# A log-softmax over rows of 50000: one row on eight partitions, fp32 in place, eight buffers, transfers from SyncE

## The chip, the cores and the metric

The kernel runs on one core of a Trainium2 chip; the other cores are idle. The metric is the device time of one execution in microseconds (us), as the slowest core shows it; with one core there is only that one. Wherever two kernels are compared, each was run on the same chip in alternation with the kernel before.

## The reference

```python
batch, seq, vocab = 16, 512, 50000          # x: fp32, 1638.4 MB
max_x = np.max(x, axis=-1, keepdims=True)
shifted = x - max_x
log_sum_exp = np.log(np.sum(np.exp(shifted), axis=-1, keepdims=True))
return (shifted - log_sum_exp).astype(np.float32)
```

There are 8192 rows of 50000 values. Each row needs its maximum, then the sum of its exponentials, then a subtraction from every value. Every byte is read once and written once if a row stays on the chip in between.

## The kernel before

A tile is 128 whole rows, one row per partition, held as bf16 (100 KB per partition, two such tiles). The load converts on its way, and so does the store.

```python
res_pool = ctx.enter_context(tc.tile_pool(name="res", bufs=2))
for it in range(ntiles):                                   # 64 tiles of 128 rows
    xres = res_pool.tile([P, V], bf16)
    for j in range(4):
        nc.gpsimd.dma_start(out=xres[:, c0:c0+LOAD_C], in_=xf[...])   # 128x12500, fp32 -> bf16
    # ... four reduce_max on VectorE, one more over the four: negmax
    for j in range(20):
        nc.scalar.activation(out=scratch, in_=xres[...], func=Exp,    # 128x2500
                             bias=negmax, accum_out=psum[:, j:j+1])
    # ... reduce_sum, Ln (another table), neglse = negmax - logsum
    for j in range(4):
        nc.scalar.activation(out=xres[...], in_=xres[...], func=Identity, bias=neglse)
        nc.gpsimd.dma_start(out=of[...], in_=xres[...])               # bf16 -> fp32
```

## Time and profile before

| | before |
|---|---|
| median time | 9335.58 us (9335.44 to 9335.72, 3 runs) |
| ScalarE (ACT) busy | 6053.9 us, 65% |
| VectorE (DVE) busy | 3400.9 us, 36% |
| DMA engines | 82.5% of 16 engines' span |
| HBM traffic | 1638.4 MB read, 1638.4 MB written |

Read it from the bottom: the traffic is fixed by the task, the DMA engines are the busiest unit, and yet they are not busy all the time. The question is when they are idle and what they then wait for.

### The profile page before, as it was taken

To read this page: it belongs to the slowest core of one execution; us is meant where nothing else is said; L and a number is where in the kernel's file an instruction comes from. 1 tells how busy PE (TensorE), PEld (TensorE's weight loads), DVE (VectorE), ACT (ScalarE), POOL (GpSimd) and SP (SyncE) were. 2 spreads that over 40 slices of the span, in tenths; PEclk is the share of its full clock that TensorE was granted. 3 is DMA by queue.
4 is the path that set the end of the run, shared out by engine and by line. 5 is a ranking of instruction groups with operands and counts; after the bars stand their busy time and mean duration, and the time that the engine had idled before them with its cause. 6 is when DMAs were issued, how large, how long until landed. Compare 5 with 4: busy or idle time off the path is not lost.

```text
span 9333.9 us, 4650 instructions
## 1 busy us (share of the span) xinstructions
DVE 3400.9 (36%) x448; ACT 6053.9 (65%) x3008; POOL 272.8 (3%) x516
## 2 busy tenths in 40 slices
DVE  4432334323344234442344423444224442243422
ACT  6556865568655686556865568655686556865568
POOL 0000000000000000000000000000000000000000
DMA  8797787977879778898778987789877888778886
GB/s 230 237 299 276 262 245 242 295 276 265 240 246 289 278 267 237 250 285 281 271 230 257 278 285 271 226 261 274 286 276 223 264 267 290 276 223 267 261 293 255
DMA packets 73765, 2457.94 MB, mean 263 GB/s; under 512 B 8192, under 2 KB 8192, under 8 KB 8192
## 3 DMA queue, kind: packets, MB, share of 16 engines
q0 software_dynamic: 73728, 2457.63, 82.5%
q14 instruction: 37, 0.30, 0.0%
HBM read 1638.40 MB, written 1638.40 MB: 351 GB/s over the span
## 4 chain that ended last, share of the span: by engine, by line
ACT 55%; DVE 18%; DMA 15%; issue 10%; another core or an unknown queue 2%; POOL 0%; ACTq 0%; POOLq 0%; PEldq 0%
ACT scratch L71 29%; ACT xres L95 26%; DVE pmax L56 18%; DMA xres<-in_x_dram 15%; ACT L83 1%; ACT L71 0%; POOL out_dram L102 0%; ACTq L131 0%; ACT logsum L83 0%; DVE neglse L91 0%; DVE negmax L63 0%; POOL xres L48 0%; POOLq L131 0%; PEldq L131 0%
## 5 line engine op out<-in xcount | busy, mean ns | idle before, releaser
L71 ACT ACTIVATE scratch<-xres,negmax 128x2500 bf16<-128x2500 bf16 x1280 | 3042.5, 2377 | 3216.6 <-DVE negmax L63 3177.9
L56 DVE TENSOR_REDUCE pmax<-xres 128x1 f32<-128x12500 bf16 x256 | 3372.5, 13174 | 2597.9 <-DMA xres<-in_x_dram 2597.9
L95 ACT ACTIVATE xres<-xres,neglse 128x12500 bf16<-128x12500 bf16 x256 | 2720.6, 10697 | 7.3 <-DVE neglse L91 7.3
L81 DVE TENSOR_REDUCE ssum<-psum 128x1 f32<-128x20 f32 x64 | 11.1, 174 | 3091.5 <-ACT scratch L71 3091.5
L102 POOL DMA_DIRECT2D out_dram<-xres x256 | 136.4, 533 | 7275.5 <-ACT xres L95 7250.2
L71 ACT ACTIVATION_READ_ACCUMULATOR scratch<-xres,negmax 128x1 f32 x1280 | 238.6, 186 | 0.0
L48 POOL DMA_DIRECT2D xres<-in_x_dram x256 | 136.4, 548 | 1752.2 <-DMA out_dram<-xres 1745.9
L71 ACT ACT_TABLE_LOAD x64 | 82.1, 1283 | 20.3 <-DMA xres<-in_x_dram 19.2
L83 ACT ACT_TABLE_LOAD x64 | 82.1, 1283 | 1.1
L91 DVE TENSOR_TENSOR neglse<-negmax,logsum 128x1 f32<-128x1 f32 x64 | 10.2, 160 | 165.9 <-ACT logsum L83 165.9
L83 ACT ACTIVATE logsum<-ssum 128x1 f32<-128x1 f32 x64 | 13.0, 203 | 0.7
L63 DVE TENSOR_REDUCE negmax<-pmax 128x1 f32<-128x4 f32 x64 | 9.7, 152 | 1.1
L120 POOL MEMSET const-float32-0.0<- 128x1 f32 x1 | 0.1, 98 | 0.2 <-issue 0.2
L120 POOL MEMSET const-bfloat16-1.0<- 128x1 bf16 x1 | 0.1, 101 | 0.0
L120 POOL MEMSET const-float32-1.0<- 128x1 f32 x1 | 0.1, 98 | 0.0
L120 POOL MEMSET const-uint8-127<- 128x1 uint8 x1 | 0.1, 98 | 0.0
## 6 DMA issues: line engine op xcount, KB each, us to landing
out_dram<-xres POOLq DMA_DIRECT2D x256, 6250.0 KB, 21.8
xres<-in_x_dram POOLq DMA_DIRECT2D x256, 3125.0 KB, 64.8
```

Of the source, the lines that this page charges most:

```text
L48: nc.gpsimd.dma_start(out=xres[:, c0 : c0 + LOAD_C], in_=xf[r0 : r0 + P, c0 : c0 + LOAD_C],)
L56: nc.vector.reduce_max(out=pmax[:, j : j + 1], in_=xres[:, c0 : c0 + LOAD_C], axis=mybir.AxisListType.X,)
L63: nc.vector.reduce_max(out=negmax, in_=pmax, axis=mybir.AxisListType.X, negate=True)
L71: nc.scalar.activation(out=scratch, in_=xres[:, c0 : c0 + C_EXP], func=mybir.ActivationFunctionType.Exp, bias=negmax, scale=1.0, accum_out ...
L81: nc.vector.reduce_sum(out=ssum, in_=psum, axis=mybir.AxisListType.X)
L83: nc.scalar.activation(out=logsum, in_=ssum, func=mybir.ActivationFunctionType.Ln, bias=0.0, scale=1.0,)
L91: nc.vector.tensor_sub(out=neglse, in0=negmax, in1=logsum)
L95: nc.scalar.activation(out=xres[:, c0 : c0 + OUT_C], in_=xres[:, c0 : c0 + OUT_C], func=mybir.ActivationFunctionType.Identity, bias=neglse ...
L102: nc.gpsimd.dma_start(out=of[r0 : r0 + P, c0 : c0 + OUT_C], in_=xres[:, c0 : c0 + OUT_C],)
L120: nc = _bacc.Bacc("TRN2", target_bir_lowering=False, num_devices=1)
```

## The change

The intent is to keep the DMA engines always at work. A row is cut into 8 pieces on 8 neighbouring partitions, so a tile is only 16 rows (128x6250 fp32, 3.2 MB, contiguous in HBM), and there are eight such buffers. Nothing is converted, and the transfers are issued by SyncE instead of GpSimd. The price is that a row's maximum and sum must be combined over 8 partitions.

```diff
+G = 8
+R = P // G
+EXP_C = 3125
+NBUF = 8
+AHEAD = 5
...
+    xt = xf.rearrange("(t r) (g w) -> t (r g) w", r=R, g=G)
+    data = ctx.enter_context(tc.tile_pool(name="data", bufs=NBUF))
...
+    # ones: 128x128, ones in 8x8 blocks on the diagonal (GpSimd, once)
+    nc.scalar.preload_act_table_set("natural_log_exp_and_others")
+    def load(t):
+        buf = data.tile([P, W], FP32, name="buf")
+        nc.sync.dma_start(out=buf, in_=xt[t])
+    def front(t):
+        nc.vector.reduce_max(out=pmax, in_=buf, axis=AX)
+        nc.vector.transpose(out=allmax, in_=pmax.to_broadcast([P, SQ]))
+        nc.vector.tensor_reduce(out=rowmax, ..., op=ALU.max, axis=AX, negate=True)
+        nc.vector.tensor_copy(out=spread..., in_=rowmax... .to_broadcast(...))
+        nc.vector.transpose(out=negmax, in_=spread)
+        for j in range(nexp):                       # 2 pieces of 3125
+            nc.scalar.activation(out=dump, in_=buf[...], func=ACT.Exp,   # dump in PSUM
+                bias=negmax[:, 0:1], scale=1.0, accum_out=part[:, j : j + 1])
+        for j in range(nexp):
+            nc.tensor.matmul(rowsum, ones, part[:, j : j + 1], ...)
+        nc.scalar.activation(out=logsum, in_=rowsum, func=ACT.Ln)
+    def back(t):
+        nc.vector.tensor_scalar(out=buf, in0=buf, scalar1=shift.pop(t)[:, 0:1],
+            scalar2=logs.pop(t), op0=ALU.add, op1=ALU.subtract)
+        nc.sync.dma_start(out=ot[t], in_=buf)
+    for t in range(AHEAD):
+        load(t)
+    for t in range(ntiles + 1):                     # 512 tiles
+        if t + AHEAD < ntiles:
+            load(t + AHEAD)
+        if t < ntiles:
+            front(t)
+        if t >= 1:
+            back(t - 1)
```

SyncE issues its transfers strictly in this order: load t+5, store t-1, load t+6, store t, and so on.

## The prediction

> **What bounds the kernel now.** I read the page top down first: busy shares, slices, DMA queues, groups.
>
> ```profile
> DVE 3400.9 (36%) x448; ACT 6053.9 (65%) x3008; POOL 272.8 (3%) x516
> ...
> DMA  8797787977879778898778987789877888778886
> ...
> q0 software_dynamic: 73728, 2457.63, 82.5%
> ...
> HBM read 1638.40 MB, written 1638.40 MB: 351 GB/s over the span
> ```
>
> No engine is full: ScalarE (ACT) is at 65%, VectorE (DVE) at 36%, the DMA engines at 82.5%. So either something rotates between them, or one of them is full only in stretches. The byte counts matter: the queue carried 2457.63 MB because a load of 6.4 MB of fp32 lands as 3.2 MB of bf16, but HBM still gave and took 1638.40 MB each way, 3276.8 MB in all. Next I read which groups were idle, and for what.
>
> ```profile
> L71 ACT ACTIVATE scratch<-xres,negmax 128x2500 bf16<-128x2500 bf16 x1280 | 3042.5, 2377 | 3216.6 <-DVE negmax L63 3177.9
> L56 DVE TENSOR_REDUCE pmax<-xres 128x1 f32<-128x12500 bf16 x256 | 3372.5, 13174 | 2597.9 <-DMA xres<-in_x_dram 2597.9
> L95 ACT ACTIVATE xres<-xres,neglse 128x12500 bf16<-128x12500 bf16 x256 | 2720.6, 10697 | 7.3 <-DVE neglse L91 7.3
> L48 POOL DMA_DIRECT2D xres<-in_x_dram x256 | 136.4, 548 | 1752.2 <-DMA out_dram<-xres 1745.9
> ```
>
> Four waits close a circle: exp waits 3177.9 us for the maximum, the maximum 2597.9 us for loads, new loads 1745.9 us for stores to free their buffer, and a store for ScalarE's last pass. Two buffers of 128 whole rows are all there is, so both tend to be loading, or both computing or storing. The chain of waits, in order of time, repeats every 290.87 us (2609.36 to 2900.23), two 128-row tiles; 32 such periods are 9308 us of the 9333.9 us span. I cut one period into stretches (columns: stretch, length, DVE, ACT, POOL busy, clock, DMA share, GB/s):
>
> ```profile
> 2653.00:2738.00 85.00, 76.97 (x7) 27.64 (x23) 0.00 (x0) 1.00 1.01 217
> 2740.00:2778.00 38.00, 13.66 (x4) 37.65 (x25) 0.00 (x0) 1.00 0.00 0
> 2780.00:2838.00 58.00, 0.00 (x0) 57.64 (x26) 1.60 (x3) 1.00 1.01 428
> 2856.00:2867.00 11.00, 9.03 (x2) 10.76 (x3) 0.00 (x0) 1.00 0.00 0
> ```
>
> While loading, the DMA engines are full (217 GB/s of bf16 landing is 434 GB/s read from HBM). While storing they are full again, at 428 GB/s. In between, for 38 us and again for 11 us, they carry nothing, and ScalarE works alone. What is lost is DMA time: this kernel is a DMA-limited one with holes.
>
> **The rate of a full DMA.** From the timeline, the maxima of consecutive load pieces start when each lands:
>
> ```profile
> 2652.41 13.18 DVE L56 TENSOR_REDUCE pmax<-xres 128x1 f32<-128x12500 bf16 x1 [72.23 <-DMA xres<-in_x_dram]
> 2667.18 13.17 DVE L56 TENSOR_REDUCE pmax<-xres 128x1 f32<-128x12500 bf16 x1 [1.59 <-DMA xres<-in_x_dram]
> 2682.00 13.17 DVE L56 TENSOR_REDUCE pmax<-xres 128x1 f32<-128x12500 bf16 x1 [1.65 <-DMA xres<-in_x_dram]
> 2696.73 13.17 DVE L56 TENSOR_REDUCE pmax<-xres 128x1 f32<-128x12500 bf16 x1 [1.56 <-DMA xres<-in_x_dram]
> ```
>
> 2667.18 to 2696.73 is two pieces, 14.78 us each; over the first seven (19.18 to 107.70, six steps) it is 14.75 us for 6.4 MB, or 434 GB/s. The period holds 16 transfers (8 loads, 8 stores) of 6.4 MB on the HBM side: 16 x 14.75 = 236 us of 290.87. The other 55 us are the two holes and their edges, and 32 x 55 = 1760 us is about what a kernel without holes could save.
>
> **What the Trainium skill says.** "DMA: Bandwidth & Descriptors", section "Where 436 GB/s comes from", puts the ceiling of the path into SBUF at 435 GB/s; the 434 above agrees. The same page, section "Latency and other measured facts", gives copies from HBM and back 214 GB/s per direction at full rate, so 428 together: loads and stores share one budget. The trace before agrees in its store stretch but scarcely mixes the two. "VectorE: DVE Perf Modes", section "The perf-mode tier table", has a reduction at one element per cycle in any type, and tensor_scalar on fp32 in SBUF at two. The trace agrees on the first (12500 elements in 13174 ns, so 0.96 per ns and some 153 ns fixed); nothing in it shows the second. "ScalarE: Activation LUTs", section "Table sets: the hidden batching unit", says one set holds both exp and ln; before, the trace pays 128 table loads of 1283 ns, 164 us.
>
> **The change, part by part** (per new tile: 16 rows, 128x6250 fp32, 3.2 MB; 512 tiles).
>
> DMA: still 1638.4 MB each way, since the old conversion saved only the SBUF side. One load and one store are 6.4 MB together: 14.75 us at the old load rate, 512 x 14.75 = 7552 us.
>
> VectorE: maximum 6250/0.96 + 153 = 6.66 us. Four small operations of 152 to 174 ns (the small reductions before), with waits about 0.8 us. The subtraction moves here from ScalarE: at two elements per cycle 3255 ns + some 160 = 3.4 us. Sum 10.9 us, below 14.75; 512 x 10.9 = 5580 us busy, some 73%.
>
> ScalarE: the four Identity passes (2720.6 us) go. An exp of 3125 elements costs 2377 + 625 x 0.833 = 2.90 us (slope from 10697 - 2377 ns over 10000 elements, 0.832), and its accumulator read 0.19; two of each 6.2 us, the Ln 0.2: 6.4 us per tile, 3270 us, some 43%. Table loads fall to one. The exp's output goes to PSUM, which may change its fixed part by tens of ns; it is off the path.
>
> TensorE: two 128x1 products per tile sum the 8 partial sums and spread them. I guess 1 us of latency, hidden.
>
> Does a wait replace the one removed? A tile's chain is 7.5 us front, 6.4 us exponentials, about 1 us of sums and Ln, and the subtraction, which VectorE does after the next tile's front: some 20 us. A load is issued five tiles ahead, and waits for the store of the tile three back. When that store lands, the queue still holds one load and one store, 14.75 us of transfers, and the new load needs only some 2 us to be issued and start. The store that follows it has long been computed. So the queue never runs dry. At the start seven loads are queued, 52 us, while the first store is ready after about 30 us. At the end, when the last load lands, some five stores are still queued (37 us) and the last tile's chain is shorter than that. Fill and drain therefore add only first and last latencies, about 5 us.
>
> Sum: 7552 + 5 = 7557 us if mixed transfers run at 434 GB/s. At the 428 of the store stretch, 3276.8 MB take 7656 us. The page's busy share (82.5% of 9333.9 us for 3276.8 MB) makes 425.5 GB/s, 7701 us. Rows of 25000 B rather than 50000 mean twice the descriptors per byte, and direction changes every 7.4 us; I allow a little for each and take 7620 us, or 430 GB/s.
>
> **Rivals.**
> 1. VectorE becomes the bound. If the subtraction runs at one element per cycle it costs 6.7 us and VectorE needs 14.1 us per tile, 7240 us at 95% busy: still just under DMA, with little slack, so 7600 to 7800 us. Doubled small-operation overheads on top would pass DMA: 7700 to 7900. For it: no such fp32 operation in the trace. Against: the tier table.
> 2. Alternating loads and stores is slower than either alone, say 400 GB/s: 8190 us. For it: the trace has long one-way stretches only. Against: the last of four stores and the next load followed each other at the usual pace (first store issued about 2577, landing of the load after all four at 2652.4: five transfers in 75 us, 15 us each), and the 214 GB/s above.
> 3. Loads and stores overlap in the engines, as they use opposite directions of HBM and SBUF; then the time would fall to VectorE's 5600 to 6500 us. Against: the 428 GB/s total above, and shares already at 1.01 in one-way stretches.
> 4. Ordering: loads and stores sit in one in-order SyncE queue, so a load waiting for an old store could hold back a ready one. For it: the program order. Against: the 14.75 us of work queued behind. If it bites, a hole of 1 to 3 us per tile: 8000 to 9000 us.
>
> **Range and chances.** The first sum's rates give 7557 to 7706 us with drain. Rival 1 lies within or just above, 2 and 4 in a tail of one in ten together, 3 about 3%. So 7620 us, with 7540 to 7770 eight times in ten. Being slower needs a loss of 1700 us, more than any rival but the worst makes: faster 0.97, same 0.015, slower 0.015.
>
> **What would show it.** DMA near 10 tenths in every slice and some 430 GB/s throughout; 3276.8 MB on the SyncE queue; VectorE near 73% with the subtraction at about 3.4 us and waiting mainly for loads; ScalarE near 43% with one table load; new loads waiting for old stores, without an empty stretch. A subtraction of 6.7 us would show rival 1, a full DMA at under 415 GB/s rival 2, holes in the DMA share rival 4.

## The result, and the profile after

The changed kernel took 7898.29 us in the median of 4 runs (7884.30 to 7910.61); before took 9335.65 beside it. The ratio is 0.846, with a 95% interval from 0.8448 to 0.8472. (Ratios here are the mean time of one kernel's fast runs over that of the other's fast runs of the same rounds, so not quite the ratio of the medians that are quoted.) It is faster, but 278 us above the predicted 7620, and above the range that ended at 7770. It also varies: 26 us between its fastest and slowest run, against 0.3 us before.

The page of the changed kernel: busy times, then of the 40 equal slices the DMA share in tenths and the GB/s moved, then the SyncE queue.

```profile
PE 600.4 (8%) x2048; PEld 513.0 (6%) x2048; DVE 5566.8 (70%) x3072; ACT 3152.9 (40%) x2561; POOL 1.2 (0%) x7
...
DMA  9999999999999999999999999999999999999999
GB/s 416 426 430 431 431 431 431 431 431 431 431 430 431 429 428 410 410 403 409 409 406 403 404 405 408 407 408 405 409 408 401 406 403 413 408 405 406 406 405 385
...
q1 hardware_dynamic: 147456, 3276.87, 99.9%
```

The holes are gone: every slice has 9 tenths. The third line is the surprise. For 15 slices, some 2960 us, the kernel moves the 430 GB/s that were predicted (a little less in the first two); then it drops within about one slice to some 406 and stays there. The DMA share gives no hint of it. Two windows put numbers on it (columns: stretch, length, busy times of PE, PEld, DVE, ACT and POOL with their instruction counts, clock, DMA share, GB/s):

```profile
1000.00:2600.00 1600.00, 126.23 (x431) 107.81 (x431) 1164.79 (x643) 661.36 (x538) 0.00 (x0) 1.00 1.00 431
3200.00:7800.00 4600.00, 342.43 (x1168) 292.55 (x1168) 3173.53 (x1748) 1797.37 (x1460) 0.00 (x0) 1.00 1.00 406
```

At 406 GB/s, 4600 us carry 1868 MB, which at 431 would have taken 4333 us: 267 us lost here, about the whole distance to the prediction. The groups, answering to those shown of before:

```profile
L81 DVE TENSOR_REDUCE pmax<-buf 128x1 f32<-128x6250 f32 x512 | 3411.6, 6663 | 2231.9 <-DMA buf<-in_x_dram 2231.9
L102 ACT ACTIVATE dump<-buf,negmax 128x3125 f32<-128x3125 f32 x1024 | 2937.9, 2869 | 4370.9 <-DVE negmax L96 4354.4
L117 DVE TENSOR_SCALAR buf<-buf,negmax,logsum 128x6250 f32<-128x6250 f32 x512 | 1789.8, 3496 | 4.5 <-ACT logsum L112 3.6
...
L67 ACT ACT_TABLE_LOAD x1 | 1.3, 1283 | 0.8 <-PEq L146 0.8
```

The engines do what was worked out for them. The maximum takes 6.663 us (6.66 predicted), the exp 2.869 (2.90), the subtraction 3.496 (3.4). VectorE waits 2231.9 us, all of it for loads, so it is not the bound. SyncE, which issues, waits as expected too:

```profile
SPq L75 <- DMA out_dram<-buf: 7333.8, 504, 23.6
SPq L121 <- DVE buf L117: 72.9, 6, 25.0
```

Loads (L75) wait for old stores to free their buffer, 504 times. Stores (L121) waited for VectorE only 6 times. So every transfer is ready early, the queue is held only by buffers, and still the rate falls after 37% of the run. Why there?

The timeline shows it as the time between two loads that SyncE issues, one per tile, first in the fast part and then in the slow part:

```profile
2308.29 0.33 SPq L75 DMA_DIRECT2D buf<-in_x_dram  x1
...
2323.15 0.33 SPq L75 DMA_DIRECT2D buf<-in_x_dram  x1
...
4001.13 0.33 SPq L75 DMA_DIRECT2D buf<-in_x_dram  x1
...
4017.03 0.33 SPq L75 DMA_DIRECT2D buf<-in_x_dram  x1
```

A tile takes 14.86 us in the first pair and 15.90 in the second: 1 us more per tile, with the same work and the same order.

### What the landings say

A transfer runs on 16 DMA engines, each with its own share and its own queue of work (a ring). The Trainium skill, "DMA: Bandwidth & Descriptors", section "Why a DMA increments its semaphore by 16 and not by 1", says that these engines finish independently and that the semaphore counts them. The trace agrees: it has 16 landings for each of the 1024 transfers. Their spread, the time from the first engine's landing to the last one's, is the lag of the slowest ring behind the fastest. Worked out from the landing records of the trace (median over the transfers that landed in the 100 us after each time):

```
lag in us at      300   600  1000  1500  2000  2500  3000  4000  5000  6000  7000 us
before            0.2   0.3   0.2   0.2   0.2   0.2   0.2   0.2   0.5   0.2   0.2
changed           3.9   5.2   7.3   9.1  11.6  11.5  12.7  13.6  13.4  13.6  13.0
```

Before, the rings finish together: each period has idle stretches (38 and 11 us) in which all can catch up, and there are fewer instruction fetches, of which more below (37 packets against 80). In the changed kernel they drift apart, until the lag reaches 12 to 13 us near 3000 us. There it stops growing, and there the rate falls.

That suggests theory 1. The awaited store "lands" only when the slowest ring has done its part. Behind it are two transfers, 14.75 us of work *for each ring*. A ring that is 12.7 us ahead has only 2 us of that left when SyncE hears of the landing, and a new transfer needs about that to be issued and to start (an estimate; in e6 below a tiny load landed 1.6 us after the store that it had waited for, at 1948.6 and 1947.0 us). Slack that is counted on the average ring is used up by the spread between rings.

What makes the rings drift? Up to 2900 us, the lag of the last ring behind the median one rises in clear steps of 1.0 to 1.2 us, at 944, 1213, 1481, 1764, 2032, 2301, 2569 and 2852 us. Every step shows at the landing some 4 us after one 8 KB packet of the instruction queue (309 to 376 ns each), at 940, 1208, 1477, 1760, 2028, 2296, 2565 and 2848 us. These packets bring the engines' own instructions, and the steps say that they pass through the same rings as the data. The interval is 268 us, twice 283, so 18 or 19 tiles; whose instructions they are the packets do not say. VectorE, with 6 operations per tile, is a guess so far.

The rivals: theory 2, that far parts of the two tensors disturb one another (an effect of the address); theory 3, that mixed loads and stores slow down as such, by whatever pattern they happen to fall into.

### The profile page after: what moved, and what is told of

Read it like the earlier page. It is cut to its first block, busy times and chain, and to the rows that moved or that the text cites. A ratio compares the mean times of both kernels' runs of the same rounds, so it can differ in the third digit from the quotient of the medians.

```text
span 7908.9 us, 12333 instructions
## 1 busy us (share of the span) xinstructions
PE 600.4 (8%) x2048; PEld 513.0 (6%) x2048; DVE 5566.8 (70%) x3072; ACT 3152.9 (40%) x2561; POOL 1.2 (0%) x7
## 4 chain that ended last, share of the span: by engine, by line
DMA 97%; SPq 1%; DVE 1%; issue 0%; ACT 0%; PE 0%; ACTq 0%
DMA out_dram<-buf 97%; SPq L75 1%; DVE pmax L81 1%; DMA buf<-in_x_dram 0%; DVE buf L117 0%; ACT dump L102 0%; DVE allmax L84 0%; DVE rowmax L86 0%; DVE spread L91 0%; DVE negmax L96 0%; PE rowsum L108 0%; ACT logsum L112 0%; ACTq L102 0%
## 5 line engine op out<-in xcount | busy, mean ns | idle before, releaser
L81 DVE TENSOR_REDUCE pmax<-buf 128x1 f32<-128x6250 f32 x512 | 3411.6, 6663 | 2231.9 <-DMA buf<-in_x_dram 2231.9
L102 ACT ACTIVATE dump<-buf,negmax 128x3125 f32<-128x3125 f32 x1024 | 2937.9, 2869 | 4370.9 <-DVE negmax L96 4354.4
L117 DVE TENSOR_SCALAR buf<-buf,negmax,logsum 128x6250 f32<-128x6250 f32 x512 | 1789.8, 3496 | 4.5 <-ACT logsum L112 3.6
L108 PE MATMUL rowsum<-part,ones 128*128 128x1 f32 x2048 | 600.4, 362 | 7269.8 <-ACT dump L102 7269.8
L108 PEld LDWEIGHTS rowsum<-part,ones 128*128 128x128 f32 x2048 | 513.0, 311 | 7357.1 <-ACT dump L102 7335.3
L102 ACT ACTIVATION_READ_ACCUMULATOR dump<-buf,negmax 128x1 f32 x1024 | 190.8, 186 | 0.0
L96 DVE STREAM_TRANSPOSE negmax<-spread 128x32 f32<-128x32 f32 x512 | 108.2, 211 | 17.7
L84 DVE STREAM_TRANSPOSE allmax<-pmax 128x32 f32<-128x32 f32 x512 | 108.2, 211 | 17.5
L86 DVE TENSOR_REDUCE rowmax<-allmax 128x4 f32<-128x32 f32 x512 | 95.3, 186 | 17.8
L91 DVE COPY spread<-rowmax 128x32 f32<-128x32 f32 x512 | 92.9, 181 | 17.8
```

Source lines behind the costliest of these rows:

```text
L81: nc.vector.reduce_max(out=pmax, in_=buf, axis=AX)
L84: nc.vector.transpose(out=allmax, in_=pmax.to_broadcast([P, SQ]))
L86: nc.vector.tensor_reduce(out=rowmax, in_=allmax.rearrange("p (r g) -> p r g", g=G), op=ALU.max, axis=AX, negate=True,)
L91: nc.vector.tensor_copy(out=spread.rearrange("p (r g) -> p r g", g=G), in_=rowmax[:, :, None].to_broadcast([P, SQ // G, G]),)
L96: nc.vector.transpose(out=negmax, in_=spread)
L102: nc.scalar.activation(out=dump, in_=buf[:, j * EXP_C : (j + 1) * EXP_C], func=ACT.Exp, bias=negmax[:, 0:1], scale=1.0, accum_out=part[:, ...
```

## The experiments

All kernels are the changed kernel with the edit shown. All gave correct results except e8.

| run | edit | median us (range) | ratio to before |
|---|---|---|---|
| changed kernel | | 7898.29 (7884.30 to 7910.61) | 0.8460 |
| e1 | tiles in reverse order | 7905.78 (7887.76 to 7937.61) | 0.8472 |
| e3 | lookahead 6 | 9760.87 (9750.20 to 9769.78) | 1.0455 |
| e2 | lookahead 4 | 7674.69 (7666.69 to 7679.62) | 0.8220 |
| e5 | lookahead 3 | 7645.33 (7643.27 to 7646.24) | 0.8189 |
| e9 | lookahead 2 | 7772.52 (7736.25 to 7787.42) | 0.8320 |
| e4 | 6 memsets per tile on VectorE | 7982.71 (7977.28 to 7988.96) | 0.8551 |
| e7 | 6 memsets per tile on GpSimd | 8026.63 (8025.42 to 8047.46) | 0.8603 |
| e10 | the same, paced by the tiles | 7907.87 (7895.19 to 7926.23) | 0.8477 |
| e6 | three full stops | 7674.79 (7673.52 to 7675.68) | 0.8221 |
| e8 | loads alone | 3846.8 (one look) | |

### e1: is it the address?

```diff
-        nc.sync.dma_start(out=buf, in_=xt[t])
+        nc.sync.dma_start(out=buf, in_=xt[ntiles - 1 - t])
-        nc.sync.dma_start(out=ot[t], in_=buf)
+        nc.sync.dma_start(out=ot[ntiles - 1 - t], in_=buf)
```

> The tiles are visited from the last to the first, nothing else changes. In the changed kernel the rate falls from 431 to about 406 GB/s near 2900 us and stays there. Theory 1 (ring drift: one of the 16 DMA engines falls behind the others by about 12 us, until the two transfers queued behind the awaited store are used up): the fall comes at about 2900 us again, 7890 to 7920 us in all. Theory 2 (address: loads and stores at the far part of the tensors disturb one another): the slow 406 GB/s comes first and the fast 431 last, with the change at about 5000 us. Theory 3 (mixing as such): no clear order; the step would move or vanish.

The rate by slices:

```profile
GB/s 417 426 429 431 430 431 430 431 431 431 430 429 431 430 427 407 406 407 408 406 405 405 407 406 408 406 403 409 409 404 407 411 406 404 407 407 405 408 406 388
```

The fast part is first again, and the fall comes in the same slice, although the tensors are now walked from the far end. Theory 2 falls.

### e2, e3: how much work lies behind the awaited store?

```diff
-AHEAD = 5
+AHEAD = 4        # e2;   6 in e3
```

With lookahead a, load t+a needs the buffer of tile t+a-8, and the last store issued by then is that of tile t-2. Behind the awaited store there are 6-a pairs of a load and a store: none for 6, two transfers for 5, four for 4, six for 3.

> Loads are issued four tiles ahead instead of five; still eight buffers. A load then waits for the store of four tiles back, with four transfers (29.5 us) queued behind it instead of two. Theory 1 (ring drift, growing at some 3.7 us per 1000 us): the rate stays near 430 GB/s until the lag reaches about 27 us, at 6700 us or later; 7640 to 7680 us in all. Theories 2 (address) and 3 (mixing): the fall near 2900 us stays and the time is 7890 to 7920 us.

> Loads are issued six tiles ahead; a load waits for the store of two tiles back, with one transfer (7.4 us) queued behind it. Theory 1 (ring drift): the fall comes when the lag reaches about 5 us, at 500 to 1300 us, and the time is 7980 to 8080 us. Theories 2 and 3: 7890 to 7920 us, fall near 2900 us as before, since the queue is as deep on average as it was.

e2, then e3, by slices, and a window of e3 with the columns of the windows above:

```profile
GB/s 416 426 431 431 430 430 431 431 431 431 431 431 430 431 431 431 431 430 431 430 431 431 431 431 430 431 431 431 431 431 431 431 430 430 430 430 428 415 410 365
```

```profile
GB/s 357 336 335 334 334 340 334 338 332 337 335 334 334 336 335 335 334 334 336 333 338 335 339 331 335 336 334 335 335 337 340 334 333 333 337 337 334 337 338 351
```

```profile
1000.00:9000.00 8000.00, 491.92 (x1676) 420.36 (x1676) 4555.52 (x2514) 2579.18 (x2095) 0.00 (x0) 1.00 0.88 335
```

e2 met the expectation closely, 7674.69 us where 7640 to 7680 was expected. The fall moved from 2960 us to about 7000, where the lag was 26.7 us: four transfers are 29.5 us, less the 2 us for a new start. A smaller lookahead, fewer loads in flight, is the faster kernel, which is the reverse of what the name suggests.

e3 was missed: it is slower than the kernel before, and I had expected 7980 to 8080. I had counted one transfer behind the awaited store; by the rule above there is none, as the load that I counted was issued ahead of that store. With none, all rings run dry once per tile. A tile takes 9761 / 512 = 19.1 us against 6.4 MB / 431 GB/s = 14.85, so a round trip through SyncE per tile costs about 4.2 us. Some 2.3 us of them are idle rings (the DMA share falls to 0.88); the rest is slower packets (mean of a 25000-byte packet 1046 ns from 1000 to 9000 us, against 931 in the fast part of the changed kernel), to which the last part comes back. The lag is 1.1 us in the median, since the rings are lined up each time.

### e4: do instruction fetches make the drift?

```diff
+    pad = consts.tile([P, 1], FP32, name="pad")
...
             back(t - 1)
+            for _ in range(6):
+                nc.vector.memset(pad, 0.0)
```

> Six tiny memsets per tile are added to VectorE, which idles some 4 us per tile; nothing else changes. In the trace of the changed kernel the lagging engine falls back by 1.0 us once every 268 us, at the time of one 8 KB instruction fetch, which is 18 tiles of VectorE instructions. If the instruction fetches of VectorE make the drift, the steps come about every 140 us, the lag grows about 1.9 times as fast and the fall comes at 1400 to 1800 us; 7960 to 8000 us in all. If the drift has another cause (a slower engine as such), the fall stays near 2900 us and the time is 7890 to 7920 us.

```profile
GB/s 417 428 430 429 431 430 430 430 424 412 407 407 406 405 406 409 404 407 411 407 406 406 403 405 406 408 405 406 407 406 408 407 401 403 406 406 413 410 409 387
...
q14 instruction: 88, 0.72, 0.0%
```

The small memsets raise VectorE's busy time by 153 us (5566.8 to 5719.8), inside its idle time. Yet the kernel is slower by 84 us, because the fall now comes in the ninth slice, at about 1700 us. Instruction packets rose from 64 to 88. The steps of the slowest ring follow: 795, 944, 1094, 1243 and 1393 us, 150 us apart, 1.1 to 1.25 us each. So the steps follow VectorE's instruction count, and they set the pace of the drift.

### e7 and e10: the same instructions on another engine

```diff
+            for _ in range(6):
+                nc.gpsimd.memset(pad, 0.0)                           # e7
...
             front(t)
+            nc.gpsimd.tensor_copy(out=pad, in_=shift[t][:, 0:1])     # e10, waits for the tile
+            for _ in range(5):
+                nc.gpsimd.memset(pad, 0.0)
```

> The same six tiny memsets per tile as in the padded run on VectorE, but on the idle GpSimd. If the instruction fetches of each engine go over one DMA ring of their own, GpSimd's steps set another ring back (every 21 tiles, about 320 us) and the largest lag is still VectorE's: fall near 2900 us, 7880 to 7930 us. If they go over the same ring as VectorE's, or the extra traffic of any fetch counts, as the padded VectorE run: fall at 1400 to 1800 us and 7960 to 8000 us.

> In the earlier padded run on GpSimd nothing paced the memsets: all 24 instruction fetches fell into the first 610 us, and the lag reached 12 us there instead of at 2900 us. Here the first of six small GpSimd instructions per tile waits for the tile's maximum, so they are spread over the run as VectorE's were. If each engine's fetches go over a ring of their own, GpSimd's ring falls back by 0.5 to 1.0 us every 320 us, no faster than VectorE's 1.0 us every 268 us: fall near 2900 us (2500 to 3000), 7890 to 7930 us. If GpSimd's fetches share VectorE's ring: fall at 1400 to 1800 us, 7960 to 8000 us, as the padded VectorE run.

e7, then e10, by slices:

```profile
GB/s 419 429 427 411 402 404 409 407 411 408 410 409 404 406 410 406 407 412 411 411 414 412 407 406 404 409 410 409 405 406 406 405 404 404 408 408 408 405 405 389
```

```profile
GB/s 418 429 430 429 431 431 431 431 430 432 430 431 430 431 431 411 418 405 409 406 406 405 407 403 407 406 409 407 407 408 410 410 407 407 406 407 408 404 408 389
```

e7 was missed, and the miss is instructive. Nothing made the memsets wait for the tiles, so GpSimd ran through all 3072 of them in the first 610 us, with a fetch every 26 us. The slowest ring was 12.6 us behind at 600 us, and the fall came there, in the fourth slice. So fetches of another engine do the same to a ring. Paced by the tiles (e10), the same number of instructions leaves the fall in the sixteenth slice and the time at 7907.87, as expected if GpSimd's fetches set back another ring than VectorE's: on one ring the two series of fetches would add up. But GpSimd's ring is not a harmless second. In e10 the steps of the slowest ring come every 239 us (16 tiles), at 1061, 1299, 1538 and 1777 us for instance, each some 4 us after a packet of an instruction series that the changed kernel does not have (1057, 1295, 1534, 1772 us); VectorE's series, every 268 or 284 us, runs beside it (908, 1176, 1460 us). So here GpSimd's ring is the last one, and it falls back about as fast as VectorE's did, which is why the time is the same.

### e6: stop everything, three times

```diff
+        if t in (128, 256, 384):
+            nc.sync.dma_start(out=stored[-1][:, 0:1], in_=xt[0][:, 0:1])
         if t + AHEAD < ntiles:
```

The tiny load overwrites one column of a buffer whose store was issued last, so SyncE must wait until that store has landed on all rings; the buffer is loaded anew later, and the result stays right.

> Five ahead as in the changed kernel, but at tiles 128, 256 and 384 a tiny load into the buffer stored last makes SyncE wait until every ring has finished all that was issued. Drift theory: each stop costs the lag of some 7 us and a restart of about 4 us, and sets the lag back to under 1 us, so it never reaches the 12 us at which the rate falls: 7660 to 7740 us, faster than the changed kernel although three full stops were added. If the 406 GB/s are a matter of address, time or mixing, the stops only cost: 7900 to 7960 us.

```profile
GB/s 417 429 430 431 430 431 431 431 431 431 400 427 429 430 431 431 431 431 431 431 400 428 429 430 430 431 431 431 431 431 398 428 430 430 431 430 431 431 431 413
```

Three added stops make the kernel 224 us faster. The slices 11, 21 and 31 show each stop, and the slow state never comes. At the stops the lag goes from 10.6, 9.7 and 11.5 us to some 1 us in the transfers that follow. This rules out time and address as causes, and leaves the lag. What the rate does just after a stop is shown in the last part.

### e5 and e9: the other side of the lookahead

```diff
-AHEAD = 5
+AHEAD = 3        # e5;   2 in e9
```

> Loads are issued three tiles ahead; a load waits for the store of five tiles back, with six transfers (44 us) queued behind it. With four ahead the lag of the slowest ring reached 26.6 us at about 5700 to 6200 us, and the rate fell only in the last three of forty slices. Drift theory: 44 us are never used up (the lag grows by some 3.7 us per 1000 us, under 32 us at the end), so no fall at all, 431 GB/s to the last slices, 7635 to 7665 us. If the depth merely helps by smoothing and has an optimum at four, or if computing now comes too close behind the loads (a store's tile has only some 31 us between load and use), 7690 us or more.

> Loads are issued two tiles ahead. Eight transfers now lie behind the store that a load's buffer needs, but the other side becomes short: a store is issued some 11 us after the slowest ring has landed the load of the next tile, with four transfers (29.5 us) queued behind that load, so about 29.5 - 11 - 2 = 16 us of lag are allowed. With three ahead the lag reached 15.9 us at 3590 us and the allowance by the same sum was 31 us, just enough. Drift theory: the rate falls from 431 to about 406 GB/s near 3600 us, 7820 to 7900 us in all. If buffers behind the awaited store were all that counts, two ahead is as good as three or better: 7635 to 7650 us.

e5, with what SyncE waited for, then e9:

```profile
GB/s 416 426 428 430 430 431 431 431 431 431 431 431 431 431 430 431 431 431 431 431 430 431 431 431 431 431 431 431 431 431 431 431 431 431 431 431 431 430 431 374
```

```profile
SPq L121 <- DVE buf L117: 7166.2, 512, 26.0
```

```profile
GB/s 417 427 429 429 431 431 431 431 431 431 431 431 431 431 431 431 431 430 430 427 414 413 415 413 414 416 413 414 414 415 414 415 413 413 415 415 413 415 415 380
```

At lookahead 3 there is no fall. The lag grows through the whole run, to 30.8 us at 7000, and costs nothing. SyncE now waits at the stores instead of at the loads, 7166.2 us. That wait costs nothing here, since six transfers are queued. It was close, though: by the sum that e9 tests, the computing leaves an allowance of 44 - 11 - 2 = 31 us at lookahead 3, and the lag reached 31.4 us at 7400. A longer run could well have met its fall (an estimate, not tried).

At lookahead 2 the allowance is set by the computing: a store can be issued only about 11 us after the slowest ring has landed the next tile's load. The fall comes where the lag reaches about 17 us (16 by the sum), near 3850 us (3600 expected). The time, 7772.52, is 47 us under the expected range, because the rate after the fall is 414 GB/s and not 406. So the place of the fall follows from the sum of the queued work; its depth does not.

### e8: is 431 what mixing costs?

The diff is shortened; its first line stands for all that was cut out.

```diff
-    # maximum of all columns, statistics, exponentials, subtraction
+        nc.vector.reduce_max(out=pmax, in_=buf[:, 0:625], axis=AX)
-        nc.sync.dma_start(out=ot[t], in_=buf)
+        if t % 128 == 127:
+            nc.sync.dma_start(out=ot[t], in_=buf)
```

> Wrong result on purpose: all 512 loads, four stores, a maximum over a tenth of each tile and nothing else, so that loads alone pace it. My prediction's first term was 14.75 us per 6.4 MB (434 GB/s), taken from long one-way stretches of 50000-byte rows; the changed kernel made 431 at its best. If mixing directions costs the difference, loads alone make 434 GB/s: 512 loads of 3.2 MB in 3775 us, about 3800 us with the four stores. If the shorter rows of 25000 bytes cost it, 431 GB/s or less: 3830 us.

A window, without the columns of PE and PEld, which have nothing to do here:

```profile
100.00:3700.00 3600.00, 386.72 (x481) 0.00 (x0) 0.00 (x0) 1.00 1.00 431
```

Loads alone run at the same 431 GB/s as loads and stores in turn. Turning from loads to stores costs nothing that shows here, once the rings are spread out. The 0.7% from 434 to 431 belongs to the shorter rows or to the other kind of queue; which, was not tried.

## Why the prediction was wrong

The direction, the mechanism of the gain and, as long as the rings are spread out, the rate were right; one step of the queue argument failed, and it was worth 253 us (7898.29 against 7645.33 at lookahead 3).

- **The bound before.** "This kernel is a DMA-limited one with holes" held: no conversion, pass or table load that left mattered in itself. ("ScalarE works alone" in the holes is not quite so: the lines shown have VectorE busy for 13.66 of 38 us and 9.03 of 11.) The DMA rows in every slice of the changed kernel show that the holes were closed.
- **The engines.** The per-tile costs came out as worked out (VectorE 70% for 73%, ScalarE 40% for 43%). VectorE had the slack it was said to have; rival 1 did not come.
- **The rate.** 430 GB/s was the chosen middle, 431 the measured rate, in the first 37% of the changed kernel and in nearly all of e5, which took 7645.33 us, 25 over the predicted 7620. Part of that is luck: 430 was a little taken off for direction changes and shorter rows, and the direction changes took nothing once the rings were spread (431 GB/s with them and, in e8, without). Also, "the 434 above agrees" with the ceiling of the path into SBUF compares unlike things: of the 434 read from HBM only 217 GB/s landed in SBUF before. The test came with e8, where 431 land, just under that ceiling.
- **The step that failed** is this: "When that store lands, the queue still holds one load and one store, 14.75 us of transfers, and the new load needs only some 2 us to be issued and start. ... So the queue never runs dry." It treats the 16 rings as one. The store lands with the slowest ring, but the 14.75 us count for the fastest, and the two drifted 12.7 us apart, so the rings ahead do run dry: after the fall (3200 to 7800 us) fewer than 16 packets are in flight for 5% of the time, in the fast part (1000 to 2600 us) for none. In its place the runs showed: the allowance is the queued work minus some 2 us, 12 to 13 us at lookahead 5 (fall at 2960 us), about 27 at 4 (fall near 7000 us), over 30 at 3 (none); and three stops that undo the drift also undo the fall.
- **Rival 4 came nearest, with the wrong look and size.** It named the order in the SyncE queue and dismissed it with the same 14.75 us. It foresaw a hole of 1 to 3 us in every tile, and "holes in the DMA share". In truth a tile grew from 14.85 to 15.76 us (6.4 MB at 431 and at 406 GB/s), only from about the 200th tile on, and the share stayed at 1.00. My sign to look for would have missed it, and the GB/s row shows it.
- **Rival 2 came in part, by its own sign**, "a full DMA at under 415 GB/s": that is what the last 63% of the run look like. As it was worded, that alternating loads and stores is slower, it is refuted by the 431 GB/s of e5 to the end. What holds of it comes next. Rival 3 did not come.

**Where the lost time lies.** Hardly in idle rings: the busy share, to a third digit, goes from 1.004 (1000 to 2600 us) to 0.999 (3200 to 7800 us). It is the packets. A packet of 25000 bytes takes 928 ns in the median before and after the fall, but the mean rises from 931 to 982 ns, or 5.4%: a tenth of them now take over 1.08 us, the slowest hundredth over 1.8 us. The share counts a packet that is held up as busy.

These slow packets go with rings that are lined up. After the fall, 15 of the 16 rings land within some 2 to 3 us of each other, so that they turn from loads to stores at the same moment. The same can be seen where no ring waits: soon after the start of the changed kernel (lag 0.8 to 1.4 us), and after each stop of e6. Windows of the changed kernel, then of e6 after its first stop, then of e8 (without PE and PEld):

```profile
50.00:100.00 50.00, 5.86 (x20) 5.01 (x20) 49.44 (x26) 28.82 (x25) 0.00 (x0) 1.00 1.00 414
100.00:150.00 50.00, 4.69 (x16) 4.01 (x16) 39.84 (x25) 24.62 (x20) 0.00 (x0) 1.00 1.00 419
```

```profile
1950.00:2000.00 50.00, 3.52 (x12) 3.00 (x12) 32.41 (x19) 18.26 (x16) 0.00 (x0) 1.00 1.01 415
2000.00:2050.00 50.00, 4.70 (x16) 4.01 (x16) 33.41 (x19) 22.00 (x20) 0.00 (x0) 1.00 1.00 418
2400.00:2800.00 400.00, 31.66 (x108) 27.05 (x108) 290.49 (x163) 166.20 (x135) 0.00 (x0) 1.00 1.00 430
```

```profile
100.00:700.00 600.00, 65.12 (x81) 0.00 (x0) 0.00 (x0) 1.00 1.00 431
```

After the stop the rate climbs from 415 to 430 GB/s as the lag grows from 1.2 to 4.8 us, with the rings full all the while. Loads alone lose nothing at a lag of 1.3 us. So rings that are lined up and turn between loads and stores are slower by some 3 to 4% without any wait; once they are spread, turning costs nothing.

What stays open: the link between the two. That the wait for the slowest ring is what lines up the other rings fits all runs, but no run tests it by itself. Nor is it shown why the rate after the fall is 406 GB/s at lookahead 5 and 414 at 2; at 2, 14 rings land within some 4 us and the other two some 18 us after the first, and the mean packet takes 967 ns. Nor was it tried what, besides the fetches, adds to the spread of the middle rings. The Trainium skill's page "DMA: Bandwidth & Descriptors", section "Queues, rings and completion order", does name a queue row, 14, for the runtime's own work on the same engines; the 64 instruction packets of queue 14 in this trace fit that, while the 16 of queue 8 are outside that row.

## What to carry to other kernels

Count the work queued behind a wait for the ring that is furthest ahead, not for the average one: a transfer lands with its slowest ring, and in a stream without pauses the rings drift apart, here by about 4 us per 1000 us. So with a fixed number of buffers, place the wait in the middle between the old store and the coming use; here lookahead 3 of 8 beat 5 by 3.2% (7645.33 us against 7898.29) with one constant, with an allowance that just sufficed for a run of this length. And when a profile says that the DMA is full, read the GB/s by slices before believing that it is as fast as it can be.

## What the Trainium skill lacked or had wrong

- "DMA: Bandwidth & Descriptors" does not say what an engine's instruction fetch costs a running stream: here one 8 KB fetch of 0.31 to 0.38 us set its ring back by 1.0 to 1.2 us, every 268 or 283 us for VectorE, and doubling VectorE's operations moved the fall from 2960 to about 1700 us. ("Runtime: NRT & Kernel Launch" treats instruction fetch too, but not what it does to data transfers.)
- The same page explains that the 16 engines finish independently, but gives no size for how far they drift: 0.2 to 0.5 us in a kernel with pauses, 30.8 us at 7000 us in one without (e5).
- No page says how much must be queued behind a completion that the next transfer waits for. Here nothing behind it cost 4.2 us per tile (e3), 14.75 us of work lasted for 2960 us of run, 44 us (with the computing's limit of 31) for the whole run.
- No page says that loads and stores in turn are slower while the 16 rings are lined up: 414 to 419 GB/s at a lag of about 1 us, 431 once spread, and 431 for loads alone at a lag of 1.3 us (e8).
- "VectorE: DVE Perf Modes", section "The perf-mode tier table", gives tensor_scalar two elements per cycle for fp32 in SBUF, but does not say whether two operations with two per-partition operands keep it. Here they did: 3496 ns for 6250 elements, where one element per cycle took 6663 ns (the maximum).
